# First layer's modulation in two steps of eight blocks per group, with own buffers for each half, and partial sums turned by transposes

## The chip, the cores and the metric

The kernel runs on one core of a Trainium2 chip. The metric is the device time of one execution in microseconds; the figure given is the median of three runs. A core has TensorE (matrix products), VectorE and ScalarE (elementwise work), GpSimd, and SyncE, which here only issues DMAs. The engines run their own instruction queues in order and wait for one another by semaphores.

## The reference

Two layers of a diffusion backbone work on 256 latent and 256 context tokens of width 2048. Each layer modulates its input by the conditioning vectors, multiplies it by one combined projection, runs a spatial gating path and an attention path, and ends with an output projection and a gated residual. What the change touches is the modulation of layer 0: shift and scale of 2048 features each, for two conditioning vectors, and the projection that consumes them.

```python
def rms_norm(x, w):
    xf = x.astype(jnp.float32)
    y = xf * lax.rsqrt(jnp.mean(xf * xf, axis=-1, keepdims=True) + EPS)
    return (y * w.astype(jnp.float32)).astype(x.dtype)

def modulation(cond, w_mod, b_mod):
    m = jax.nn.silu(cond) @ w_mod + b_mod
    m = m.reshape(-1, 1, 3 * D_MODEL)
    return jnp.split(m, 3, axis=-1)
...
        shift, scale, gate = modulation(c, w_mod[layer], b_mod[layer])
        shift_c, scale_c, gate_c = modulation(c_ctx, w_mod[layer], b_mod[layer])
        h = rms_norm(x, norm_w[layer]) * (1.0 + scale) + shift
        hc = rms_norm(xc, norm_w[layer]) * (1.0 + scale_c) + shift_c
...
        proj = h @ w_in[layer]
        u, v_sgu, za, q, k, v, zb = jnp.split(proj, SPLIT_POINTS, axis=-1)
```

## The kernel before

Every large product runs as three passes over exact splits of both operands (`three`: hi*hi, lo*hi, hi*lo). The order of work on TensorE, SyncE, VectorE and ScalarE is the program's own order.

Layer 0 begins with the key, value and query columns of the projection, 1536 of them, and takes the 2048 contraction rows in nine groups of 128-row blocks: `GROUPS` is (0,), (1,), (2, 3), (4, 5), up to (14, 15). For each group the kernel must first have the shift and scale of its features (a `ModItems` object), then the modulated rows (`rows_h`), and then it multiplies them by the group's three pieces of weights. `run_groups` goes through the groups. Each pass but the first has twelve calls of `group_unit`, u = 0 to 11: for each of three column pieces `ci` and four token tiles `tt`, six products of 512 columns (three where the group has one block) into one of four accumulators of the pool `accp`. VectorE then adds the accumulator to the result in SBUF. `first_group` does the same for group 0 while the context tokens still arrive.

Between the units of group gi the kernel prepares group gi + 1:

- `mod_step` at u = 0, 2, 4 and 6 (`WAVE[0]`): four contraction blocks of the modulation product. Each block's weights are the moving operand, 512 columns (256 for a group of one block), and the two conditioning vectors, padded to 32 columns, are the stationary one. The four blocks of a step write four strips of 32 partitions of one PSUM bank, so four partial sums stand there in the end. After the last step ScalarE copies them to `part`.
- `finish` at u = 8 (`WAVE[1]`): TensorE multiplies 128-column pieces of `part` with the constant `sel`, which adds the four strips and turns features onto the partitions; `mod_ab` makes the factors A and B.
- `rows_h` at u = 10 and 11: the modulated rows of the latent and the context tokens.
- `load_w` at u = 2, 4 and 7 (`LOADS`) issues the three weight pieces of group gi + 1, 512 KB each; `split_w` at u = 2, 3 and 8 (`SPLITS`) makes hi by a cast on ScalarE and, a tick later, lo by a subtraction on VectorE. The split at u = 2 is that of the third piece of group gi, the other two belong to group gi + 1.

SyncE issues all these loads. The modulation weights, 4 MB for a group of two blocks, come in pieces of 512 KB into the six rotating buffers `raw`, which `load_w` uses for its third piece too; `mod_load` keeps at most `MOD_AHEAD` of them counted ahead, and one step (`MOD_BIG`) has a buffer of its own. Of the loads that stand before `load_w(gi + 1, 0)` in a pass, those issued at u = 0 and u = 2 are modulation pieces for the steps that follow. The pool tag `pt`, two buffers of 1 MB, is first used by attention, after the last group.

Of the kernel before, what the change touches and what calls it, by code (L numbers as in the profile page):

```python
# [49 lines left out]
FIRST = ((0, 1), 0, (3, 4, 6), 5, (9, 11), (7, 11))  # L50
LOADS = (2, 4, 7)
SPLITS = (2, 3, 8)
WAVE = ((0, 2, 4, 6), 8, 10)
AHEAD = {'raww': 3, 'rawm': 3}
MOD_AHEAD = 3
MOD_BIG = (8,)
# [7 lines left out]
def mixer_kernel(ctx: ExitStack, tc: tile.TileContext, a, out):  # L64
    """Tokens are ordered latent (tiles 0, 1), context (tiles 2, 3).

    Every large product runs as three float32r passes over exact splits of both
    operands: v = hi + lo with hi = float32r(v), and a*b = hi*hi + hi*lo + lo*hi.
    """
# [56 lines left out]
    sel = const([P, 2], "sel")  # L126
    G.dma_start(out=sel, in_=a["sel"])
# [9 lines left out]
    # the conditioning vectors behind their SiLU, in rows: (quarter, stream, element)  # L137
# [23 lines left out]
    def consts_task(l, L):  # L161
        """What the mixer needs beside the modulation: norm weights, and those of queries and keys with the rotation."""
        vn = const([P, 8], "vn")
        nc.sync.dma_start(out=vn, in_=a["vnt"][l])
        L["vn"] = vn
        cs = t2([P, 2, 2, HD], "cs")
        nc.sync.dma_start(out=cs, in_=a["cossin"])
        ws = []
        for key, wname in (("k", "k_norm_w"), ("q", "q_norm_w")):
            w = const([P, HD], "w" + key)  # L170
            load_bc(w, a[wname][l])
            ws.append(w)
        yield 8
        V.tensor_scalar(out=ws[1], in0=ws[1], scalar1=HD ** -0.5, scalar2=None, op0=ALU.mult)
        for key, w in zip("kq", ws):
            C = const([P, NLAT, HD], "C" + key)
            Sn = const([P, NLAT, HD], "S" + key)
            wb = view(w, "p (o d) -> p o d", o=1).broadcast_to([P, NLAT, HD])
            V.tensor_tensor(out=C, in0=cs[:, 0], in1=wb, op=ALU.mult)
            ws4 = view(w, "p (x h d) -> p x h d", x=2, h=2)  # L180
            for h in range(2):
                for n in range(NLAT):
                    V.tensor_tensor(
                        out=view(Sn[:, n], "p (x h d) -> p x h d", x=2, h=2)[:, :, h],
                        in0=view(cs[:, 1, n], "p (x h d) -> p x h d", x=2, h=2)[:, :, h],
                        in1=ws4[:, :, 1 - h], op=ALU.mult)
                yield 1
            L["w" + key], L["C" + key], L["S" + key] = w, C, Sn

# [7 lines left out]
    def split_piece(rs, at_once, mem=None):  # L197
        """float32r parts of two contraction blocks; the second part follows a tick later unless at once."""
# [13 lines left out]
    class ModItems:  # L212
        """Shift and scale of n blocks of features from block kt0, for both streams, on the tensor engine: four
        steps over the contraction, then a finish."""

        def __init__(self, L, kt0, n):
            self.L, self.kt0, self.n, self.wd, self.raw = L, kt0, n, 2 * n * P, {}

        def load(self, g, mem=None):
            kt0, n, wd = self.kt0, self.n, self.wd  # L220
            per = 1024 // wd
            self.raw[g] = []
            for k in range(4 * g, 4 * g + 4, per):
                r = view(mem() if mem else raw2(None), "p a (b n) -> p (a b) n", n=wd)
                o = 2 * P * D * kt0 + k * P * wd
                nc.sync.dma_start(out=r, in_=view(a["w_mod0"][o:o + per * P * wd], "(k p n) -> p k n", p=P, n=wd))
                self.raw[g] += [r[:, j, :] for j in range(per)]

        def compute(self, g):
            wd = self.wd  # L230
            if g == 0:
                self.ps = misc("mod")
            for j in range(4):
                T.matmul(self.ps[32 * j:32 * j + 32, :wd], sc[:, 4 * g + j, :], self.raw[g][j],  # L234
                         start=(g == 0), stop=(g == 3))
            if g == 3:
                self.part = t2([P, 512], "part")[:, :wd]
                (S.copy if PART_ACT else V.tensor_copy)(self.part, self.ps[:, :wd])

        def finish(self):  # L240
            n = self.n
            p2 = view(misc("ab")[:, 0:8], "p (j c) -> p j c", c=2)
            for j in range(2 * n):
                T.matmul(p2[:, j, :], self.part[:, j * P:(j + 1) * P], sel, start=True, stop=True)
            mod_ab(self.L, p2[:, :n], p2[:, n:2 * n], self.kt0, n)
# [10 lines left out]
    def mod_task(row0, ng, ns, pace, finish):  # L256
        """ng groups of 256 columns of the modulation product on the vector engine, columns on the partitions.
        finish gets the sums [P, 2 * ng, ns] of the first ns streams."""
# [42 lines left out]
    def mod_rest():  # L301
        """The gates of the first layer, then the second layer's modulation."""
# [5 lines left out]
    # A task is a generator; it yields how many units of the main stream pass before it goes on.  # L308
# [5 lines left out]
    def later(k, f):  # L314
        """Emit f's instructions k + 1 ticks from now."""
# [27 lines left out]
    class Job:  # L343
        """512 output columns: units of main-stream work for each piece of two contraction blocks."""
# [38 lines left out]
    class Stream:  # L383
        """The pieces of a list of jobs in order, loaded and split ahead of their use."""
# [50 lines left out]
    def head_norm(q, n, kind):  # L435
        """q [P, n, 128] in place: divide by the root mean square of each head."""
# [41 lines left out]
    def attention_task(L, kv, qa, units, done):  # L478
        """kv [P, 4, 512]: k heads in columns 0..255, v heads in 256..511. qa[hf] [P, nt, 4, 128]: queries in,
        transposed attention output in the same place."""  # L480
# [152 lines left out]
    def gate_evac(func, buf, ntok, mix=None):  # L633
        """buf [P, nt, 4, 128] *= func(product), block fb of 128 features; split if that was the last factor."""
# [13 lines left out]
    def to_mix(buf, mix, fb):  # L648
        """Split block fb of a finished [P, nt, 4, 128] buffer into float32r parts [P, 4, tokens]."""
# [6 lines left out]
    def sgu_v(L, buf, hf, nt):  # L656
        """buf [P, nt, 4, 128] gets the position-mixed value path, transposed."""
# [57 lines left out]
    def modulate(L, kt, stream, xs, rb, hi, lo):  # L715
        """hi + lo = xs * rb * A + B for one block of 128 features; returns what makes lo."""
# [7 lines left out]
    # column starts of the combined projection  # L724
    U0, VS0, ZA0, Q0, KV0, ZB0 = 0, 1024, 2048, 3072, 4096, 4608

    # ================= layer 0 =================
    L0 = layer_consts(0)
    mods = [ModItems(L0, g[0], len(g)) for g in GROUPS]
    mseq = [(m, g) for m in mods for g in range(4)]  # L730
    mpos = [0, 0]

    def mod_load():
        """Loads modulation weights ahead, into at most MOD_AHEAD buffers."""
        while mpos[0] < len(mseq):
            m, g = mseq[mpos[0]]
            own = mpos[0] in MOD_BIG
            if not own and mpos[1] + m.n > MOD_AHEAD:
                return
            if own:  # L740
                t_ = big([P, 4, NTOK], s="mod")
                m.load(g, iter((t_[:, :2], t_[:, 2:])).__next__)
            else:
                m.load(g)
                mpos[1] += m.n
            mpos[0] += 1

    def mod_step(m, g):
        m.compute(g)
        if m is not mods[0] and mseq.index((m, g)) not in MOD_BIG:  # L750
            mpos[1] -= m.n
        mod_load()
# [4 lines left out]
    def stats(s, g):  # L757
        """Mean squares of a stream's tokens; the tensor engine adds up over the features on the partitions."""
# [20 lines left out]
    for g in range(4):  # L779
        if g % 2 == 0:  # L780
            first = big([P, 4, NTOK], s="mod")
        mods[0].load(g, lambda: first[:, 2 * (g % 2):2 * (g % 2) + 2, :])
    mpos[0] = 4
# [26 lines left out]
    def rows_h(gi):  # L810
        """Space for the modulated rows of a group, and the steps that make them."""
# [17 lines left out]
    mod_load()  # L829
    mod_step(mods[0], 0)  # L830
    mod_step(mods[0], 1)
    dg0 = stats_rows(0)
    mod_step(mods[0], 2)
    mod_step(mods[0], 3)
# [10 lines left out]
    def first_group():  # L845
        """The latent tokens' products run while the other stream arrives."""
        for u, (ci, tt) in enumerate([(ci, 2 * s + t) for s in range(2) for ci in range(3) for t in range(2)]):
# [4 lines left out]
            if u in FIRST[2]:  # L852
                mod_step(mods[1], FIRST[2].index(u))
            if u == FIRST[3]:
                dg1 = stats_rows(1)
            if u == 6:
                mod_step(mods[1], 3)
# [28 lines left out]
    def run_groups():  # L886
        first_group()
        for gi in range(1, len(GROUPS)):
            nxt = mods[gi + 1] if gi + 1 < len(GROUPS) else None
            make = []  # L890
            for u in range(3 * NT):
                if nxt and u in WAVE[0]:
                    mod_step(nxt, WAVE[0].index(u))
# [67 lines left out]
    # the residual stream is read again for the output projection  # L961
# [42 lines left out]
    # layer 1 jobs  # L1004
# [78 lines left out]
    # last columns of layer 0: the latent tokens end first, so that their next layer can begin  # L1083
# [18 lines left out]
    def next_task(s):  # L1102
        """The next layer's input of one stream, from the new residual stream."""
# [63 lines left out]
    # ================= layer 1 =================  # L1167
# [6 lines left out]
def _layout(inputs):  # L1174
# [22 lines left out]
    # constants of the shapes alone  # L1197
# [33 lines left out]
```

## Time and profile before

| | |
|---|---|
| median of three runs | 1196.34 us (1195.98 to 1197.25) |
| span of the profiled execution, first to last instruction | 1194.6 us |
| TensorE (PE) busy | 1169.5 us, 98% |
| VectorE (DVE) busy | 908.9 us, 76% |
| ScalarE (ACT) busy | 521.5 us, 44% |
| moved by DMA | 247.52 MB, 207 GB/s in the mean |

The profile is of one execution, and its time is the span and what lies before and after it; no clock of that execution but the span is given, and the median of the runs is 1.74 us above it. PE, PEld, DVE, ACT and POOL are the engines' names in the rows (PEld is TensorE's loading of the stationary operand), SPq is SyncE's queue. Matrix products are pipelined: a record of 0.39 us is followed by the next one's start after 0.23 us, so starts are to be compared, not ends. A fp32 product that isn't split leaves two records. A row of windows gives the stretch and its length, then the busy time (and the count of instructions) of PE, PEld, DVE, ACT and POOL, the granted clock of TensorE (1.00 is 2.4 GHz), the busy share of the DMA engines and their GB/s.

### The profile page before, as it was taken

Reading aid. Unit: us, or ns where it says so; the run is one execution under the profiler, and the core shown is the slowest. Engines: PE = TensorE matmul, PEld = TensorE weight load, DVE = VectorE, ACT = ScalarE, POOL = GpSimd, SP = SyncE. Lnnn points to the kernel's source line nnn. Section 1 sums busy time; section 2 is a strip of 40 time slices with the busy share of each in tenths; the row PEclk is TensorE's granted clock in tenths of the full one; section 3 lists DMA queues with packets and bytes.
Section 4 is the critical chain, followed back from the end, with each engine's and each line's share of the span. In section 5 each row is a group of like instructions: output and inputs, shape, how many; then the busy total and the mean of one; then the engine's idle time right before and its main releaser. Section 6 shows DMA issues by size and latency. Waiting matters only on the chain.

```text
span 1194.6 us, 18034 instructions
## 1 busy us (share of the span) xinstructions
PE 1169.5 (98%) x6656; PEld 991.5 (83%) x6656; DVE 908.9 (76%) x1930; ACT 521.5 (44%) x992; POOL 47.0 (4%) x48
## 2 busy tenths in 40 slices
PE   4999999999999999999999999999999999999998
PEld 2566667888888888888888888987888989999998
DVE  5767769878887777989988998778558687767544
ACT  4422225565555432242332232146366777645332
POOL 1000001011000000010100000000011000000000
PEclk9999999999999999999999999999999999999999
DMA  9986772446354657677786666646456666677752
GB/s 334 345 291 246 264 290 99 145 130 191 117 159 141 178 179 224 192 232 219 253 299 215 215 203 195 229 118 220 139 161 200 216 195 220 207 258 252 236 190 89
DMA packets 132184, 247.52 MB, mean 207 GB/s; under 512 B 8912, under 2 KB 19696, under 8 KB 132096
## 3 DMA queue, kind: packets, MB, share of 16 engines
q1 hardware_dynamic: 130880, 242.08, 62.3%
q0 software_dynamic: 1216, 4.29, 1.0%
q8 instruction: 52, 0.85, 0.3%
q14 instruction: 36, 0.29, 0.1%
HBM read 244.23 MB, written 2.11 MB: 206 GB/s over the span
## 4 chain that ended last, share of the span: by engine, by line
PE 89%; DVE 4%; ACT 3%; issue 1%; SPq 1%; POOL 1%; DMA 1%; POOLq 0%; ACTq 0%; DVEq 0%
PE acc L339 27%; PE acc L341 26%; PE acc L340 26%; PE mod L234 2%; PE tp L544 1%; DVE lo L205 1%; PE sg L686 1%; PE s L341 1%; ACT hi L202 1%; PE o L340 1%; PE o L341 1%; PE o L339 1%; POOL rs L429 1%; PE s L340 1%; PE s L339 1%
## 5 line engine op out<-in xcount | busy, mean ns | idle before, releaser
L202 ACT CAST hi<-raw 128x1024 fp32r<-128x1024 f32 (+1 forms) x242 | 250.7, 1036 | 395.6 <-PE acc L340 283.2
L205 DVE TENSOR_TENSOR lo<-raw,hi 128x1024 fp32r<-128x1024 f32 (+1 forms) x242 | 292.2, 1208 | 126.8 <-ACT hi L202 126.5
L284 DVE SCALAR_TENSOR_TENSOR junk<-raw,scb 128x512 f32<-128x512 f32 x448 | 308.1, 688 | 14.5 <-DMA raw<-in_w_modt 5.5
L339 PE MATMUL acc<-hh,hi 128*128 128x512 f32 x384 | 152.6, 397 | 0.0
L341 PE MATMUL acc<-hh,lo 128*128 128x512 f32 x384 | 149.8, 390 | 0.0
L340 PE MATMUL acc<-hl,hi 128*128 128x512 f32 x384 | 149.8, 390 | 0.0
L339 PE MATMUL acc<-hi,hh 128*128 128x512 f32 x320 | 131.0, 409 | 3.1 <-ACT hh L720 3.1
L341 PE MATMUL acc<-hi,hl 128*128 128x512 f32 x320 | 125.6, 393 | 0.0
L340 PE MATMUL acc<-lo,hh 128*128 128x512 f32 x320 | 125.3, 392 | 0.0
L339 PE MATMUL acc<-h,hi 128*128 128x256 f32 x384 | 110.3, 287 | 1.0 <-ACT s L660 1.0
L341 PE MATMUL acc<-h,lo 128*128 128x256 f32 x384 | 108.6, 283 | 0.0
L340 PE MATMUL acc<-h,hi 128*128 128x256 f32 x384 | 108.5, 283 | 0.0
L339 PE MATMUL acc<-mh,hi 128*128 128x512 f32 (+1 forms) x304 | 106.5, 350 | 0.0
L341 PE MATMUL acc<-mh,lo 128*128 128x512 f32 (+1 forms) x304 | 106.4, 350 | 0.0
L340 PE MATMUL acc<-ml,hi 128*128 128x512 f32 (+1 forms) x304 | 106.4, 350 | 0.0
L339 PEld LDWEIGHTS acc<-hi,hh 128*128 128x128 f32 x320 | 60.5, 189 | 38.8 <-issue 14.7
L341 PEld LDWEIGHTS acc<-hh,lo 128*128 128x128 f32 x384 | 72.1, 188 | 15.4
L340 PEld LDWEIGHTS acc<-hl,hi 128*128 128x128 f32 x384 | 72.3, 188 | 13.5
L339 PEld LDWEIGHTS acc<-hh,hi 128*128 128x128 f32 x384 | 72.2, 188 | 13.5
L429 POOL TENSOR_TENSOR rs<-rs,nhalf 128x4 f32<-128x4 f32 (+1 forms) x36 | 40.9, 1137 | 892.7 <-DVE rs L428 892.7
L340 PE MATMUL acc<-lo,h 128*128 128x512 f32 x192 | 75.3, 392 | 0.7 <-DVE lo L205 0.3
L339 PE MATMUL acc<-hi,h 128*128 128x512 f32 x192 | 75.7, 394 | 0.0
(163 smaller groups left out, 2166.6 us busy)
## 6 DMA issues: line engine op xcount, KB each, us to landing
raw<-in_w_in SPq DMA_DIRECT2D x173, 512.0 KB, 4.4
raw<-in_w_modt SPq DMA_DIRECT2D x128, 512.0 KB, 4.7
raw<-in_w_out SPq DMA_DIRECT2D x64, 512.0 KB, 5.0
raw<-in_w_mod SPq DMA_DIRECT2D x58, 512.0 KB, 6.2
scb<-crow SPq DMA_DIRECT2D x12, 512.0 KB, 6.0
xT<-in_xT SPq DMA_DIRECT2D x8, 512.0 KB, 7.8
x<-in_xT POOLq DMA_DIRECT2D x4, 1024.0 KB, 11.0
mod<-in_w_mod SPq DMA_DIRECT2D x6, 512.0 KB, 7.7
```

Of the source, the lines that this page charges most:

```text
L202: S.copy(hi, rs)
L205: V.tensor_tensor(out=lo, in0=rs, in1=hi.bitcast(F32), op=ALU.subtract)
L234: T.matmul(self.ps[32 * j:32 * j + 32, :wd], sc[:, 4 * g + j, :], self.raw[g][j], start=(g == 0), stop=(g == 3))
L284: V.scalar_tensor_tensor(out=junk, in0=rs[i][:, b_, :], scalar=1.0, in1=scbs[q][:, s_, :], op0=ALU.mult, op1=ALU.mult, accum_out=part[:, 2 ...
L339: T.matmul(ps, lhi, rhi, start=first, stop=False)
L340: T.matmul(ps, lhi, rlo, start=False, stop=False)
L341: T.matmul(ps, llo, rhi, start=False, stop=last)
L429: G.tensor_tensor(out=r, in0=r, in1=nhalf[:, :n], op=ALU.pow)
L544: T.transpose(out=tp[:, c * P:(c + 1) * P], in_=p_[:, c * P:(c + 1) * P], identity=ident)
L686: T.matmul(ps[:, tt * P:(tt + 1) * P], buf[:, tt, g, :], ws[:, g, :], start=True, stop=True)
```

## The change

The modulation of each group now runs in two steps of eight contraction blocks, at u = 2 and u = 6. Blocks k and k + 4 write the same strip, so there are still four partial sums. Each half has its own buffers: the first half of a group's weights lies in the two `pt` buffers (two DMAs of 1 MB), the second in four `raw` buffers (four DMAs of 512 KB). For group 1, with one block, it is one DMA of 1 MB into a buffer of `u8` and two of 512 KB. `mod_step(i, h)` computes half h of group i and then loads half h of group i + 1 into the buffers that it has just read. `finish` turns `part` by transposes, 128 columns each, and VectorE adds the four strips by one reduce out of PSUM. The constant `sel` and its DMA go. `LOADS` and `SPLITS` stay as they are. Comments and docstrings that the diff removes are left out here.

```diff
-FIRST = ((0, 1), 0, (3, 4, 6), 5, (9, 11), (7, 11))
+FIRST = ((0, 1), 0, 4, 5, (9, 11), (7, 11))
 LOADS = (2, 4, 7)
 SPLITS = (2, 3, 8)
-WAVE = ((0, 2, 4, 6), 8, 10)
+WAVE = ((2, 6), 8, 10)
-MOD_AHEAD = 3
-MOD_BIG = (8,)
...
-    sel = const([P, 2], "sel")
-    G.dma_start(out=sel, in_=a["sel"])
...
+        def load(self, mem):
+            wd, k = self.wd, len(self.raw)
+            per = mem.shape[1] // wd
+            r = view(mem, "p (k n) -> p k n", n=wd)
+            o = 2 * P * D * self.kt0 + k * P * wd
+            nc.sync.dma_start(out=r, in_=view(a["w_mod0"][o:o + per * P * wd], "(k p n) -> p k n", p=P, n=wd))
+            self.raw += [r[:, j, :] for j in range(per)]
+
+        def compute(self, ks):
             wd = self.wd
-            if g == 0:
+            if ks[0] == 0:
                 self.ps = misc("mod")
-            for j in range(4):
-                T.matmul(self.ps[32 * j:32 * j + 32, :wd], sc[:, 4 * g + j, :], self.raw[g][j],
-                         start=(g == 0), stop=(g == 3))
-            if g == 3:
+            for k in ks:
+                j = 32 * (k % 4)
+                T.matmul(self.ps[j:j + 32, :wd], sc[:, k, :], self.raw[k], start=k < 4, stop=k >= KT - 4)
+            if ks[-1] == KT - 1:
                 self.part = t2([P, 512], "part")[:, :wd]
                 (S.copy if PART_ACT else V.tensor_copy)(self.part, self.ps[:, :wd])
 
         def finish(self):
             n = self.n
-            p2 = view(misc("ab")[:, 0:8], "p (j c) -> p j c", c=2)
+            pt = misc("ab")[:, :self.wd]
             for j in range(2 * n):
-                T.matmul(p2[:, j, :], self.part[:, j * P:(j + 1) * P], sel, start=True, stop=True)
-            mod_ab(self.L, p2[:, :n], p2[:, n:2 * n], self.kt0, n)
+                T.transpose(out=pt[:, j * P:(j + 1) * P], in_=self.part[:, j * P:(j + 1) * P], identity=ident)
+            ab = small([P, 4, 2], "ab")[:, :2 * n]
+            V.tensor_reduce(out=ab, in_=view(pt, "p (j a b) -> p j b a", a=4, b=32)[:, :, 0:2, :], axis=AX.X, op=ALU.add)
+            mod_ab(self.L, ab[:, :n], ab[:, n:2 * n], self.kt0, n)
...
-    def mod_step(m, g):
-        m.compute(g)
-        if m is not mods[0] and mseq.index((m, g)) not in MOD_BIG:
-            mpos[1] -= m.n
-        mod_load()
+    def mod_load(i, h):
+        m = mods[i]
+        for _ in range(1 if h == 0 and m.n == 1 else 2 * m.n if h else 2):
+            if h:
+                mem = view(raw2(None), "p a b -> p (a b)")
+            else:
+                mem = view((big if i == 1 else ptile)([P, 4, 512], F32, s="mod"), "p a b -> p (a b)")
+            m.load(mem)
+
+    def mod_step(i, h, ahead=1):
+        mods[i].compute(range(8 * h, 8 * h + 8))
+        if i + ahead < len(mods):
+            mod_load(i + ahead, h)
...
-    mod_load()
-    mod_step(mods[0], 0)
-    mod_step(mods[0], 1)
+    mod_load(1, 0)
+    mod_load(1, 1)
+    mods[0].compute(range(8))
     dg0 = stats_rows(0)
-    mod_step(mods[0], 2)
-    mod_step(mods[0], 3)
+    mods[0].compute(range(8, KT))
...
-            if u in FIRST[2]:
-                mod_step(mods[1], FIRST[2].index(u))
+            if u == FIRST[2]:
+                mod_load(2, 0)
+                mods[1].compute(range(8))
...
             if u == 6:
-                mod_step(mods[1], 3)
+                mod_step(1, 1)
...
                 if nxt and u in WAVE[0]:
-                    mod_step(nxt, WAVE[0].index(u))
+                    mod_step(gi + 1, WAVE[0].index(u))
```

## Rows read from the trace of the kernel before

**Rows 1.** The page, busy time of the engines, share of the span, instructions.

```profile
PE 1169.5 (98%) x6656; PEld 991.5 (83%) x6656; DVE 908.9 (76%) x1930; ACT 521.5 (44%) x992; POOL 47.0 (4%) x48
```

**Rows 2.** Windows, the pass over group 4.

```profile
96.54:118.72 22.18, 22.18 (x113) 14.72 (x113) 15.01 (x27) 5.44 (x8) 0.00 (x0) 1.00 0.79 273
```

**Rows 3.** Timeline of TensorE, group 4, u = 2: start, length, engine, line, operation.

```profile
100.17 0.39 PE L341 MATMUL acc<-hi,hl 128*128 128x512 f32 x1
100.49 1.07 PE L234 MATMUL mod<-raw,scb 128*32 128x512 f32 x8
101.48 0.50 PE L339 MATMUL acc<-hi,hh 128*128 128x512 f32 x1
101.82 0.39 PE L340 MATMUL acc<-lo,hh 128*128 128x512 f32 x1
102.05 0.39 PE L341 MATMUL acc<-hi,hl 128*128 128x512 f32 x1
```

**Rows 4.** Timeline of TensorE, first group: one step of four blocks, then two together.

```profile
27.02 0.64 PE L234 MATMUL mod<-raw,scb 128*32 128x256 f32 x8
27.59 0.50 PE L339 MATMUL acc<-hi,hh 128*128 128x512 f32 x1
...
30.50 1.07 PE L234 MATMUL mod<-raw,scb 128*32 128x256 f32 x16
31.50 0.71 PE L704 MATMUL rsb<-dg,ones 128*128 128x128 f32 x4
```

**Rows 5.** Timeline of TensorE, group 4, u = 8: the finish.

```profile
112.01 0.39 PE L341 MATMUL acc<-hi,hl 128*128 128x512 f32 x1
112.24 0.95 PE L244 MATMUL ab<-sel,part 128*128 128x2 f32 x8
113.05 0.49 PE L339 MATMUL acc<-hi,hh 128*128 128x512 f32 x1
```

**Rows 6.** Timeline of TensorE, attention: four transposes between products.

```profile
224.23 0.40 PE L341 MATMUL acc<-hi,hl 128*128 128x512 f32 x1
224.46 0.60 PE L544 MATMUL tp<-ident,p 128*128 128x128 f32 x4
224.82 0.48 PE L339 MATMUL acc<-hi,hh 128*128 128x512 f32 x1
```

**Rows 7.** Timeline of VectorE, group 4, from u = 3 on.

```profile
105.66 1.22 DVE L205 TENSOR_TENSOR lo<-raw,hi 128x1024 fp32r<-128x1024 f32 x1 [1.79 <-ACT hi L202]
106.81 0.68 DVE L884 TENSOR_TENSOR kv<-acc,kv 128x512 f32<-128x512 f32 x1
...
113.22 0.16 DVE L252 TENSOR_TENSOR modB<-ab,bm 128x4 f32<-128x4 f32 x1
```

**Rows 8.** Timeline of ScalarE, group 4: modulated rows, cast of the split at u = 3.

```profile
97.50 0.91 ACT L720 ACTIVATE hh<-hm,modB 128x256 fp32r<-128x256 f32 x2 [1.55 <-DVE hm L719]
...
104.58 1.04 ACT L202 CAST hi<-raw 128x1024 fp32r<-128x1024 f32 x1 [5.23 <-PE acc L341]
```

**Rows 9.** Timeline of SyncE's queue, group 4: two issues, modulation and weights.

```profile
97.63 0.37 SPq L226 DMA_DIRECT2D raw<-in_w_mod  x1
98.05 0.46 SPq L803 DMA_DIRECT2D raw<-in_w_in  x1
```

**Rows 10.** Issue to landing by source line: issues at 97.63, 98.05 and 75.86.

```profile
DMA to landing us min/median/max: 3.7/3.7/3.7
...
DMA to landing us min/median/max: 4.5/4.5/4.5
...
DMA to landing us min/median/max: 5.9/5.9/5.9
```

**Rows 11.** Timeline of TensorE: an early product, and products after a long wait.

```profile
23.24 0.63 PE L339 MATMUL acc<-hi,hh 128*128 128x512 f32 x1
...
208.69 0.41 PE L520 MATMUL qt<-ident,qa 128*128 128x128 f32 x2 [1.77 <-DVE rs L428]
...
209.17 0.39 PE L340 MATMUL acc<-lo,hh 128*128 128x512 f32 x1
```

More of the change, by code (lines that the diff above doesn't have):

```diff
@@ L216, in __init__ @@
         def __init__(self, L, kt0, n):
[L217 to L229, printed above, removed]
+            self.L, self.kt0, self.n, self.wd, self.raw = L, kt0, n, 2 * n * P, []
+        def load(self, mem):
[6 more added lines that the diff above has]
+        def compute(self, ks):
             wd = self.wd
-            if g == 0:
+            if ks[0] == 0:
                 self.ps = misc("mod")
-            for j in range(4):
-                T.matmul(self.ps[32 * j:32 * j + 32, :wd], sc[:, 4 * g + j, :], self.raw[g][j],
-                         start=(g == 0), stop=(g == 3))
-            if g == 3:
+            for k in ks:
+                j = 32 * (k % 4)
+                T.matmul(self.ps[j:j + 32, :wd], sc[:, k, :], self.raw[k], start=k < 4, stop=k >= KT - 4)
+            if ks[-1] == KT - 1:
                 self.part = t2([P, 512], "part")[:, :wd]
@@ L729, in mixer_kernel @@
     mods = [ModItems(L0, g[0], len(g)) for g in GROUPS]
[L730 to L742, printed above, removed]
-            else:
-                m.load(g)
-                mpos[1] += m.n
-            mpos[0] += 1
-    def mod_step(m, g):
-        m.compute(g)
-        if m is not mods[0] and mseq.index((m, g)) not in MOD_BIG:
-            mpos[1] -= m.n
-        mod_load()
+    def mod_load(i, h):
[3 more added lines that the diff above has]
+                mem = view(raw2(None), "p a b -> p (a b)")
+            else:
+                mem = view((big if i == 1 else ptile)([P, 4, 512], F32, s="mod"), "p a b -> p (a b)")
[4 more added lines that the diff above has]
+            mod_load(i + ahead, h)
     sq, sums0 = [], small([P, 512], "sums", bufs=1)
@@ L781, in mixer_kernel @@
             first = big([P, 4, NTOK], s="mod")
-        mods[0].load(g, lambda: first[:, 2 * (g % 2):2 * (g % 2) + 2, :])
-    mpos[0] = 4
+        mods[0].load(view(first[:, 2 * (g % 2):2 * (g % 2) + 2, :], "p a b -> p (a b)"))
     for g in range(4):
```

## The prediction

> **What bounds the kernel now.** I read the page first, then the windows by stage, then the timeline of TensorE through one wave, and last the queues that feed it. TensorE works for 98% of the span [rows 1], so a change counts only where it shortens or holds up TensorE. Call one pass of `run_groups` over a group a wave, its twelve `group_unit` calls units 0 to 11, and `load_w(gi + 1, 0)` W0. In the window of wave 4 TensorE is busy for the whole stretch, 22.18 of 22.18 us [rows 2]; waves 2, 3 and 5 to 7 have the same length within 0.1 us, and wave 1, with half the products, is as dense. So no load, split or sum holds it up there: each microsecond taken from TensorE in a wave is a gain, each new wait a loss. Before wave 1, at the start of the kernel, it does wait for others.
>
> **What TensorE gains.** A step of four blocks for two feature blocks: the last product before it starts at 100.17, the first after it at 101.48 and the second at 101.82, where two more products at their pitch of 0.23 would have ended the same distance at 100.63 [rows 3]. It costs 1.19 us, of which 0.09 is waited before it (0.32 instead of 0.23) and 0.11 after it (0.34 instead of 0.23). What lies inside shows in the first group, with half the columns: four blocks take 0.57 us to the next product, eight in a row 1.00 [rows 4]. Four more cost 0.43 there, and a step of their own would have cost 0.57 + 0.32 + 0.34 - 0.46 = 0.77. Merging two steps therefore saves 0.34. With 512 columns four more blocks cost twice 0.43, so a step of eight costs 1.19 + 0.86 = 2.05 us (and 0.99 + 0.86 = 1.86 from its start to the next product). A wave merges twice: 0.68.
>
> The finish now takes 1.04 us from the last product to the next [rows 5]; four transposes of the same size take 0.59 where attention does them [rows 6]. That saves 0.45. The new reduce on VectorE (32 numbers a partition) is bounded by the sum over 4 elements, 0.16, and by the one over 512, 0.68 [rows 7]; I take 0.2, as it is nearest to the small one. It lies behind transposes that end at unit 8, and the factors are wanted at unit 10, two units of 1.38 us later, so it costs nothing; without that cover it would cost its 0.2. Waves 1 to 7 each have a modulation group: 7 x (0.68 + 0.45) = 7.9 us gained. The steps and finishes of the first two groups lie in the start, where TensorE then waits for row statistics anyway: I count them as nothing (at most 0.34 + 2 x 0.23). The lost DMA of `sel` is off the path.
>
> **What the new order of loads costs.** SyncE issues in program order and stops at a buffer that isn't free. Before, W0 went out at 98.05, behind one modulation load of 97.63, while TensorE was still in unit 0 [rows 9]; TensorE's step at unit 2 came at 100.49. After the change, `mod_step` at unit 2 runs its eight blocks and then reloads the two `pt` tiles that those blocks have just read: two transfers of 1 MB, and W0 stands behind them in the same queue. The first `pt` tile is free when four blocks have ended, 1.07 us after the start A of the step [rows 3]. A load on an idle queue landed after 3.7 us, W0 issued 0.42 later after 4.5 [rows 9, 10]: 1.3 us per 512 KB behind 2.4 us of latency. So W0 (512 KB behind 2 MB) lands at A + 1.07 + 2.4 + 5 x 1.28 = A + 9.9; before, it landed 98.05 + 4.5 - 100.49, at A + 2.1.
>
> Who waits for it: the cast of `split_w(gi + 1, 0)` on ScalarE, emitted at unit 3. Before, it began at 104.58, when unit 3 had ended and its buffer came free [rows 8]. Behind it on VectorE stands `lo` (105.66), and behind `lo` the sum of unit 3 (106.81, 0.68 long) [rows 7]: 2.9 us from cast to the end of that sum. There are four accumulators, so unit 7 can't begin before unit 3's is added up. After the change that is A + 9.9 + 0.1 + 2.9 = A + 12.9. TensorE alone would come to unit 7 at A + 1.86 (step) + 1.48 + 3 x 1.38 + 0.09 + 1.86 (the step at unit 6) + 1.48 = A + 10.9. TensorE stands for 2.0 us in each wave that loads a following modulation group: waves 2 to 6 make 10.0. Wave 7 has nothing more to load, and W0 goes out early there.
>
> The Trainium skill, "DMA: Bandwidth & Descriptors", Specifications, puts the limit of the memory at about 358 GB/s for a core. By that figure 512 KB would take 1.46 us, W0 would land 0.9 later, and six waits would cost 5.4 more; the trace's 1.3 us is about 400 GB/s and the measurement decides.
>
> Wave 1 has units of three products (0.69), so TensorE is at unit 7 sooner: A + 1.86 + 0.80 + 3 x 0.69 + 0.09 + 1.86 + 0.80 = A + 7.5. It stands for 5.4. Then VectorE is late with the next group's rows. From A + 12.9 it has four sums (0.6 each, as a successor starts some 0.07 before the end: `lo` of 1.22 is followed after 1.15), the reduce and the factors (0.6), another `lo` (1.15), two more sums (1.2), and a product; with the activation behind it that is another 1.0, since two such activations take 0.91 [rows 7, 8]: A + 19.3 for the first `hh`. TensorE would come to wave 2 at A + 12.9 + 5 x 0.69 + 0.36 (finish) + 0.11 = A + 16.8. That is 2.4 more; bounds nothing and 3. Wave 1 loses 7.8.
>
> W0 took 5.9 us to land in wave 3, and as long in wave 2, where it took 4.5 in wave 4 [rows 10]; two in seven were late. Before, nothing waited for that. Now such 1.3 us falls on TensorE: none of six to all of six is 0 to 7.8; two in seven of six make 2.2. I take 1.5, between that and nothing.
>
> Sum: -7.9 + 10.0 + 7.8 + 1.5 = +11.4 us. The profiled span of 1194.6 becomes 1206.0; the median of the runs, 1196.34, is 1.7 above that span, and becomes 1207.7. I say 1207.5.
>
> **The rivals.** *The late load is hidden.* If W0 lands by A + 7.9, unit 7 finds its accumulator, only the gain is left, and the time is 1196.3 - 7.9 = 1188.5. For it speaks that the waves have no wait now and that the DMA engines are busy for only 0.79 of wave 4 [rows 2]; against it, the issue at A + 1.07 and the latency leave 4.4 us for 2.5 MB that take 6.4 at the rows' pace. A scheduler that issues W0 first, or a queue that serves it at once, would also do it. Chance 0.10.
>
> *The waits are half of that.* If the chain from issue to sum is 1 us shorter, the waits are 4.4 in wave 1 and 1.0 in five others, and without late landings the loss nearly equals the gain: 9.4 - 7.9 = +1.5, 1197.8, or 1200.2 with wave 1's second wait. Chance 0.08.
>
> *The waits grow, or TensorE slows after them.* Late landings in all six waves make 1207.7 - 1.5 + 7.8 = 1214. And the first products of the kernel took 0.63 us where later ones take 0.39 [rows 11]: TensorE began at 1.2 GHz, by that duration, for some seven products, which costs 7 x 0.24 = 1.7; in wave 4 the granted clock reads 1.00, 2.4 GHz [rows 2]. If each wait threw it back there, six waits cost 10 us, 1217.7; in wave 1 alone, 1209.4. The nearest row speaks against the short waits: after 1.77 us of standing at 208.69 the next products took 0.39 as before [rows 11]; for the 5.4 us of wave 1 there is no row. The Trainium skill, "TensorE: Matmul & The Clock Gate", "Why this matters for your kernels", says that an idle gap between bursts of matmuls sends the clock from 2.4 back to 1.2 GHz if it is long enough; the 1.77 us row shows no such fall, and no run here shows it for a longer one. Chance 0.16.
>
> **How the numbers follow.** The forecast has 0.66. A run of this kernel can tell about 0.2%, 2.4 us, from no change. Faster is the first rival, 0.10. Of the second rival 0.05 lies within 2.4 us of 1196.3, the rest above: same 0.05, slower 0.66 + 0.16 + 0.03 = 0.85. The low end of the range takes the waits at 1.5 us in five waves, 5.0 in wave 1 and nothing else: -7.9 + 7.5 + 5.0 = +4.6, 1201. The high end takes late landings in all waves and the slow products in wave 1: 11.4 - 1.5 + 7.8 + 1.7 = +19.4, cut to 1215, since both at full size are unlikely together. Below lie the first rival and most of the second.
>
> **What would show it.** In the windows of waves 1 to 6 TensorE must no longer be busy throughout: one wait per wave, before the first product of unit 7, released by VectorE's sum, some 2 us long (5 in wave 1), and a cast on ScalarE that waits for the DMA of `in_w_in`. The waves should last 23.1 us where they last 22.2, the last of them 21.0. Each step must show as sixteen records with about 1.86 us to the next product, each finish as four. If the waves last 21.0 with no wait, the late load was hidden and I am wrong on the sign; if the wait comes before the finish or before a step instead, the mechanism is another.

## The result and the profile after

The changed kernel takes 1223.82 us (median; 1221.28 to 1228.08) where the kernel before takes 1196.74 in the same comparison: ratio 1.0226 [1.0212, 1.0241]. The forecast was 1207.5 in a range of 1201 to 1215. The sign was right, the size far too small.

The profiled execution has a span of 1226.3 us. The page's first two parts and its chain, against [rows 1]: TensorE's busy time has hardly grown, and its clock has an 8 in two of the first slices, where the page before has a 9 in all.

```profile
PE 1174.3 (96%) x6624; PEld 997.9 (81%) x6624; DVE 909.0 (74%) x1939; ACT 521.4 (43%) x992; POOL 46.9 (4%) x47
...
PEclk9899989999999999999999999999999999999999
...
PE 82%; DMA 6%; DVE 5%; ACT 4%; SPq 2%; issue 1%; POOL 1%; ACTq 0%; POOLq 0%; DVEq 0%
```

The waits of TensorE from wave 1 to the end of the waves (engine, what waited, what released it: total us, times, longest):

```profile
PE acc L337 <- DVE kv L874: 23.8, 7, 7.2
...
PE acc L337 <- ACT hh L718: 1.0, 1, 1.0
```

L874 is VectorE's sum of a unit. The waits before unit 7 are 7.2 us in wave 1 and 2.9, 3.6, 4.1, 2.8 and 2.7 in waves 2 to 6; wave 7 has none; the seventh of the row, 0.5 us, stands before unit 6 of wave 1, and the one for `hh` at the start of wave 2. TensorE's timeline in wave 2, from the step at unit 2 to the wait (start, duration, in brackets the idle time before and its releaser), answers to [rows 3]:

```profile
65.32 1.92 PE L230 MATMUL mod<-mod,scb 128*32 128x512 f32 x16
67.17 0.50 PE L337 MATMUL acc<-hi,hh 128*128 128x512 f32 x1
...
72.88 1.92 PE L230 MATMUL mod<-raw,scb 128*32 128x512 f32 x16
...
76.02 0.39 PE L339 MATMUL acc<-hi,hl 128*128 128x512 f32 x1
79.34 0.79 PE L337 MATMUL acc<-hi,hh 128*128 128x512 f32 x1 [2.94 <-DVE kv L874]
79.93 0.63 PE L338 MATMUL acc<-lo,hh 128*128 128x512 f32 x1
80.36 0.63 PE L339 MATMUL acc<-hi,hl 128*128 128x512 f32 x1
```

Unit 6 ends with the product of 76.02, and unit 7 starts at 79.34. The chain behind it stands in the timelines of SyncE's queue, ScalarE and VectorE, and in the landing times of the three issues of 66.44, 67.30 and 67.72:

```profile
66.44 1.23 SPq L221 DMA_DIRECT2D mod<-in_w_mod  x2
67.72 1.09 SPq L793 DMA_DIRECT2D raw<-in_w_in  x2
...
76.38 1.04 ACT L198 CAST hi<-raw 128x1024 fp32r<-128x1024 f32 x1 [10.32 <-DMA raw<-in_w_in]
...
77.46 1.23 DVE L201 TENSOR_TENSOR lo<-raw,hi 128x1024 fp32r<-128x1024 f32 x1 [7.88 <-ACT hi L198]
78.60 0.68 DVE L874 TENSOR_TENSOR kv<-acc,kv 128x512 f32<-128x512 f32 x1
```

```profile
DMA to landing us min/median/max: 5.5/5.5/5.5
DMA to landing us min/median/max: 7.6/7.6/7.6
DMA to landing us min/median/max: 8.6/8.6/8.6
```

The two 1 MB transfers land at 71.9 and 74.9, W0 behind them at 76.3; the cast follows at 76.38, `lo` at 77.46, the sum of unit 3 ends at 79.28, and unit 7 begins. This is the forecast's chain, about 1 us later than it said. The second thing to see is the duration behind the wait: 0.63 and a pitch of 0.43 us instead of 0.39 and 0.23. The windows of the stretch before and behind the wait, of waves 2, 3 and 5, and of the low clock in wave 1 (columns as in [rows 2]; the seventh figure is the granted clock):

```profile
75.00:79.30 4.30, 1.40 (x6) 0.78 (x5) 1.84 (x3) 1.53 (x2) 0.00 (x0) 1.00 1.05 392
79.34:82.72 3.38, 3.38 (x10) 2.69 (x11) 2.15 (x4) 0.37 (x1) 0.00 (x0) 0.50 1.05 387
82.74:91.10 8.36, 8.36 (x39) 6.67 (x37) 7.55 (x18) 3.32 (x6) 0.00 (x0) 1.00 0.08 30
65.32:91.10 25.78, 22.85 (x110) 15.69 (x109) 15.56 (x29) 5.98 (x9) 0.00 (x0) 0.93 0.62 224
91.10:117.64 26.54, 22.92 (x110) 15.72 (x109) 15.00 (x28) 5.34 (x9) 0.00 (x0) 0.94 0.62 218
144.60:171.55 26.95, 24.19 (x109) 16.69 (x109) 16.38 (x39) 5.01 (x9) 0.00 (x0) 0.87 0.60 215
...
52.05:58.88 6.83, 3.09 (x9) 2.57 (x10) 4.74 (x10) 2.58 (x3) 0.00 (x0) 0.50 0.97 359
```

Behind each of the six waits of this execution (in waves 1, 5 and 6 already within it) the clock reads 0.50, which is 1.2 GHz, for 3.41 or 6.83 us: 27.3 us in all, of which TensorE stands for 4.7, most of it in wave 1. Working 22.6 us at half clock loses half of that, 11.3. The waves last 25 to 27 us where the forecast had 23.1.

### The profile page after: what moved, and what is told of

Read it like the earlier page. It is cut to its first block, busy times and chain, and to the rows that moved or that the text cites. A ratio compares the mean times of both kernels' runs of the same rounds, so it can differ in the third digit from the quotient of the medians.

```text
span 1226.3 us, 17941 instructions
## 1 busy us (share of the span) xinstructions
PE 1174.3 (96%) x6624; PEld 997.9 (81%) x6624; DVE 909.0 (74%) x1939; ACT 521.4 (43%) x992; POOL 46.9 (4%) x47
## 4 chain that ended last, share of the span: by engine, by line
PE 82%; DMA 6%; DVE 5%; ACT 4%; SPq 2%; issue 1%; POOL 1%; ACTq 0%; POOLq 0%; DVEq 0%
PE acc L337 25%; PE acc L339 24%; PE acc L338 24%; DMA raw<-in_w_in 5%; DVE lo L201 2%; PE mod L230 1%; ACT hi L198 1%; PE tp L542 1%; PE sg L684 1%; DMA mod<-in_w_mod 1%; PE s L339 1%; PE o L338 1%; POOL rs L427 1%; PE o L339 1%; PE o L337 1%
## 5 line engine op out<-in xcount | busy, mean ns | idle before, releaser
L201 DVE TENSOR_TENSOR lo<-raw,hi 128x1024 fp32r<-128x1024 f32 (+1 forms) x242 | 292.4, 1208 | 169.6 <-ACT hi L198 169.3
L337 PE MATMUL acc<-hi,hh 128*128 128x512 f32 x320 | 134.2, 419 | 28.3 <-DVE kv L874 23.8
L338 PE MATMUL acc<-lo,hh 128*128 128x512 f32 x320 | 129.2, 404 | 0.0
L339 PE MATMUL acc<-hi,hl 128*128 128x512 f32 x320 | 129.0, 403 | 0.0
L337 PEld LDWEIGHTS acc<-hi,hh 128*128 128x128 f32 x320 | 62.6, 196 | 56.1 <-DVE kv L874 27.3
```

Of the source, the lines that this page charges most:

```text
L201: V.tensor_tensor(out=lo, in0=rs, in1=hi.bitcast(F32), op=ALU.subtract)
L337: T.matmul(ps, lhi, rhi, start=first, stop=False)
L338: T.matmul(ps, lhi, rlo, start=False, stop=False)
L339: T.matmul(ps, llo, rhi, start=False, stop=last)
```

## The experiments

The theory after the result: W0 stands in SyncE's queue behind 2 MB, its cast and `lo` hold up the sum of unit 3 on VectorE, TensorE waits for that before unit 7, and then works at half clock for a while. Rivals: the transposes and the reduce cost the time; the loads have become slower; the clock falls for another reason than the waits. Each comparison is with the kernel before on the same chip.

**The changed kernel again** (`after_again`), without an edit.

> The changed kernel once more, as the yardstick of the three kernels run beside it on the same chip. Late load of W0 with falls of the granted clock (theory): about 1222 us, in the passes over groups 1 to 6 one wait before unit 7 of 2.9 to 4.2 us (7 in the first) and a stretch at 0.5 after each. Rival, that the profiled execution had only a slow memory: landings of 512 KB return to 1.27 to 1.30 us apart, the waits shrink to 2.0 us and the time to about 1208.

1222.92 us, ratio 1.0221 [1.0199, 1.0242]. The waits repeat (6.5, 2.7, 2.9, 3.9, 2.9 and 2.85 us), but in the profiled execution the clock fell only after those of wave 1, 4 and 6, for 13.7 us in all, and its span is 7.7 us shorter than the one shown above. That fits the changed kernel's own spread of 7 us: how often the clock falls differs from execution to execution (the mean granted clock of the eight executions is 0.987 to 0.994).

**W0 ahead of the reloads** (`w0_early`): the one load is issued a unit earlier, the rest of the change stays.

```diff
-LOADS = (2, 4, 7)
+LOADS = (1, 4, 7)
```

> One number: the first weight piece of the next group is issued at unit 1, ahead of the reload of the two 1 MB buffers. Theory (the 2 MB in front of it make it late, all loss hangs on that): the waits of groups 2 to 6 go, group 1 keeps about 2 us because its loads are still queued from the start, the granted clock stays at 1.00; 1196.7 - 7.9 + 2 + 1 = about 1192 us. Rival (the larger transfers or the shared buffers slow all loads, or the reduce and transposes are to blame): the waits stay, above 1208 us.

1198.76 us, 1.0016 [1.0007, 1.0026]: 24 of the 26 us are gone, though the 1192 expected was not reached. Waits of TensorE from wave 1 on, then the windows of waves 1 and 3:

```profile
PE acc L337 <- ACT hh L718: 4.1, 1, 4.1
...
PE acc L337 <- DVE kv L874: 1.3, 1, 1.3
```

```profile
39.35:61.80 22.45, 17.00 (x79) 10.42 (x78) 15.19 (x30) 6.14 (x10) 0.00 (x0) 0.85 0.89 328
82.80:103.86 21.06, 21.06 (x110) 14.59 (x109) 14.90 (x28) 5.46 (x9) 0.00 (x0) 1.00 0.78 275
```

Waves 2 to 6 have no wait and last 21.0 us (one 21.5), 1.1 less than before [rows 2]. What is left is in wave 1: 22.45 us where its work takes 14.2. There the second piece now stands behind the 2 MB, and the rows of group 2 come late. So the place of one issue in the queue explains nearly all of the loss.

**The splits later** (`split_late`): W0 lands late, but no sum stands behind it until unit 6.

```diff
-SPLITS = (2, 3, 8)
+SPLITS = (2, 6, 8)
```

> One number: the loads stay as in the changed kernel, W0 still lands some 11 us after the step at unit 2, but its cast and subtraction stand at unit 6 instead of unit 3. Theory (what hurts is not the late load but that ScalarE and VectorE stand behind it in their queues and hold an accumulator): no wait in groups 2 to 6, about 5 us left in group 1 with a fall of the clock; 1196.7 - 7.9 + 5 + 2 + 1 = about 1197 us. Rival (TensorE lacks data): about 1222 us as before.

1204.05 us, 1.0058 [1.0041, 1.0075]. Waits from wave 1 on:

```profile
PE acc L337 <- DVE qa L874: 4.1, 1, 4.1
PE acc L337 <- ACT hh L718: 3.9, 4, 1.5
```

The loads are as in the changed kernel, yet no wait stands before unit 7: it is not the load but the work queued behind it that held TensorE. The expectation missed by 7 us. In wave 1 the same chain, emitted three units later, held up a later sum for 4.1 us; in four waves the next group's rows (`hh`), which VectorE makes behind the split, came late by up to 1.5 us, 3.9 in all; and the clock read 0.50 for 10.2 us, from within the first wait on. One wait was spread over other places.

**The wait filled with products** (`fill_wait`): nothing that the output uses changes; before unit 7 TensorE does products that nobody reads.

```diff
+                if u == 7 and gi <= len(GROUPS) - 3:
+                    fill = misc("fill")
+                    for _ in range(28 if gi == 1 else 12):
+                        T.matmul(fill, H[GROUPS[gi][0]][0][:, 0:P], wpcs[gi, 1][0][:, 0, :], start=True, stop=True)
                 group_unit(gi, *divmod(u, NT))
```

> The changed kernel with products that nothing reads, 12 of 512 columns (28 in group 1) before unit 7 of groups 1 to 6, where TensorE would only stand. Theory (of the loss some 12 us are the half rate after each wait): the granted clock stays at 1.00, the waits end no later, and the time falls by 10 to 12 us below the changed kernel on the same chip, to about 1211. Rival (the half rate costs little, because VectorE is the bound there anyway): no gain, or a loss of up to 3 us for the added products.

1216.27 us, 1.0162 [1.0147, 1.0178]. Mean granted clock, the products that fill the wait of wave 2, the first behind them, and the wave's window:

```profile
core 0: 1214.8 us, clock 1.000
```

```profile
75.14 2.91 PE L904 MATMUL fill<-hi,hh 128*128 128x512 f32 x12
78.05 0.50 PE L337 MATMUL acc<-hi,hh 128*128 128x512 f32 x1
78.39 0.39 PE L338 MATMUL acc<-lo,hh 128*128 128x512 f32 x1
```

```profile
64.22:88.26 24.04, 24.04 (x121) 16.75 (x120) 15.37 (x29) 5.95 (x9) 0.00 (x0) 1.00 0.66 241
```

The chain to unit 7 is as late as before, but TensorE does not stand, and the clock does not fall: more work, 6.65 us less time than in the unedited kernel of the same comparison (some 3 us either way, by the two intervals; 10 to 12 was expected). The mean granted clock of its four executions is 0.999 or 1.000. So standing is what lowers the clock, and 6.65 us is about what that costs in a typical execution, where the first profile makes it 11.3; it is a net figure, as `fill_wait` waits 2.1 us for `hh` at the start of wave 2 where `after_again` waits 0.3.

**The kernel before once more** (`before_look`), and **the new finish alone** (`finish_only`): the kernel before with the transposes and the reduce in place of `sel`, and its old steps and loads.

```diff
-    sel = const([P, 2], "sel")
-    G.dma_start(out=sel, in_=a["sel"])
...
             for j in range(2 * n):
-                T.matmul(p2[:, j, :], self.part[:, j * P:(j + 1) * P], sel, start=True, stop=True)
+                T.transpose(out=pt[:, j * P:(j + 1) * P], in_=self.part[:, j * P:(j + 1) * P], identity=ident)
```

> The kernel before, profiled again beside the others. In the profiles of the changed kernel 512 KB land 1.355 us apart, already in loads that the change leaves alone, and 1.27 to 1.30 in the first profile of before. If that pace belongs to the chip or the execution, this run too shows about 1.355, and still no wait of TensorE in groups 1 to 7 (span 1194 to 1196). If the change causes it, this run shows 1.27 to 1.30.

> The kernel before with one part of the change alone: transposes and the reduce on VectorE in place of the products with sel. Theory (0.45 us less on TensorE for each of seven groups, the reduce hidden): 0.26% faster, 3.1 us, and no new wait. Rival (the reduce lengthens the way to the factors and the rows come late, as they do in the changed kernel before some groups): no gain, or up to 1.5 us slower.

The kernel before ran in 1196.67 us, with dense waves. The finish alone: 1196.04, 0.9992 [0.9983, 1.0001]. It costs nothing, so that rival falls; but it gave less than expected. Its waves are shorter as expected; its start is 0.8 us later (first product of the second half of the first group at 34.59 instead of 33.78), as in the changed kernel, and its 512 KB loads land 1.35 us apart instead of 1.28. The experiments with the pad, below, ask why.

**All weight loads first** (`w_first`, and with it the later split, `w_first_split_late`): the changed kernel with its three weight pieces issued ahead of the modulation reloads.

```diff
-LOADS = (2, 4, 7)
+LOADS = (0, 1, 2)
...
             for u in range(3 * NT):
+                if u in LOADS:
+                    load_w(gi + 1, LOADS.index(u))
                 if nxt and u in WAVE[0]:
                     mod_step(gi + 1, WAVE[0].index(u))
...
-                if u in LOADS:
-                    load_w(gi + 1, LOADS.index(u))
```

> The changed kernel with all three weight pieces of the next group issued at units 0, 1 and 2, each ahead of the reloads of modulation buffers. Theory (the loss left in w0_early is group 1 alone, where the second piece stands behind 2 MB while the queue is still full from the start): about 2 us of wait left before unit 7 of group 1, no fall of the clock, 1196.8 - 7.9 + 2 + 1 = about 1192 us. Rival (the early load of a whole group of modulation weights costs its 4 MB at the start in any order): the loss of group 1 moves to the step at unit 2 of group 2, and the time stays at about 1198.

> As w_first, and the cast of the first piece at unit 6 instead of 3. Theory: the wait of group 1 goes too, TensorE is dense from group 1 on, about 1190 us, 0.6% faster than before. Rival: as for w_first, about 1198.

`w_first`: 1194.99 us, 0.9983 [0.9974, 0.9991]; `w_first_split_late`: 1195.61, 0.9990 [0.9981, 0.9999]. No wait before unit 7 is left worth naming; the later split buys nothing: 2.8 us of waiting for `hh` at the start of wave 2 against 2.1 without it. Both lie above what was expected, again with the loads 1.35 us apart.

**Thirty-two bytes** (`after_pad`, `before_shift`, `finish_pad`, `w_first_pad`). The constant `sel`, [128, 2], takes 32 bytes of each partition. Without it the large buffers that come behind it in SBUF start 32 bytes past a multiple of 64 bytes instead of at one (by the program's own allocation; a trace shows no addresses). The edit puts an unused constant of the same size there: into three kernels without `sel`, which restores the old places, and into the kernel before, which shifts them.

```diff
+    V.memset(const([P, 2], "pad"), 0.0)
     ones = const([P, P], "ones")
```

> The changed kernel with an unused constant of two elements a partition where sel stood. It takes 32 bytes a partition, so all large buffers lie again at multiples of 64 bytes, as in the kernel before; without it they lie 32 bytes off. Theory (the offset slows every load): 512 KB land 1.27 to 1.30 us apart as before, the start ends at 33.8 again, the waits before unit 7 shrink to 2.0 to 2.5 us (5.4 in group 1), the granted clock falls less often; about 1208 to 1212. Rival (the chip or the changed loads are slow, not the addresses): 1.355 us and 1222 as before.

> The kernel before with the same unused constant added, which moves its large buffers 32 bytes off the multiples of 64. Theory: 512 KB land 1.345 to 1.355 us apart, the loads of the start 1.5 instead of 1.35, the start ends about 0.9 us later, and the time grows by 1 to 2 us. Rival: no change, 1.28 and 1196.8.

> The transposes and the reduce alone, with the large buffers at multiples of 64 bytes. Theory (in finish_only the gain of 3.2 us on TensorE was eaten by the slower loads of the start): 1197.1 - 3.2 = about 1193.9 us, 0.27% faster. Rival (the reduce delays the rows): 1196 as in finish_only.

> All weight pieces ahead of the reloads, and the large buffers at multiples of 64 bytes. Theory: the start is 1 to 2 us shorter than in w_first and the wait at the step of group 2 smaller, about 1191 to 1192 us, faster than before by 0.4 to 0.5%. Rival: 1195 as in w_first.

One window at the start, 12.6 to 21.7 us, when the loads run without a break, in the kernel before (`before_look`), the kernel before shifted, the changed kernel and the changed kernel with the pad (the last figure is GB/s):

```profile
12.60:21.70 9.10, 6.54 (x44) 3.27 (x44) 5.16 (x15) 2.18 (x5) 0.93 (x2) 1.00 1.08 389
```

```profile
12.60:21.70 9.10, 6.99 (x44) 3.54 (x44) 4.61 (x14) 1.78 (x4) 1.07 (x2) 1.00 1.09 355
```

```profile
12.60:21.70 9.10, 6.78 (x42) 3.02 (x42) 4.68 (x15) 1.78 (x4) 0.79 (x2) 1.00 1.09 355
```

```profile
12.60:21.70 9.10, 6.65 (x43) 3.25 (x38) 4.84 (x15) 3.03 (x6) 0.71 (x1) 1.00 1.08 389
```

The pace follows the place of the buffers: 389 GB/s in the old place, 355 shifted, whichever kernel it is. In time, each against the kernel before on its own chip: `before_shift` 1197.96, 1.0009 [1.0000, 1.0018], 1.0 us more; `finish_pad` 1194.21, 0.9979 [0.9970, 0.9988], 1.7 us better than `finish_only`; `w_first_pad` 1192.3, 0.9962 [0.9949, 0.9976], 2.5 us better than `w_first`. But `after_pad` takes 1223.57, 1.0220 [1.0206, 1.0234], as long as without the pad, where 1208 to 1212 was expected. Its start is faster: the second half of the first group begins at 32.95 instead of 34.63, of which 0.8 lie before TensorE's first product (11.96 instead of 12.77) and 0.9 behind it. Its waits are as long as in `after_again`:

```profile
PE acc L338 <- DVE kv L875: 21.6, 6, 6.2
```

So the slower loads don't make the waits of the changed kernel, and that rival falls for the waves; with the pad, too, W0 lands at A + 10.6 to A + 11.8 (A is the start of the step at unit 2, as in the prediction).

**The 1 MB transfers cut in two** (`after_pad_512`): `after_pad`, with the `pt` buffers loaded by four DMAs of 512 KB.

```diff
+    V.memset(const([P, 2], "pad"), 0.0)
...
-            m.load(mem)
+            if h or i == 1:
+                m.load(mem)
+            else:
+                m.load(mem[:, :1024])
+                m.load(mem[:, 1024:])
```

> As after_pad, with the two pt buffers loaded in four transfers of 512 KB instead of two of 1 MB; order and gates are the same. Theory (the prediction's sum is right once the pieces are those of its rows): W0 lands at A + 9.9 instead of A + 10.8, the waits before unit 7 are 1.9 to 2.2 us, and if TensorE's clock then stays at 1.00 after most of them, the time is about 1208 to 1211. Rival (the first megabyte of a burst is slow whatever its pieces): W0 at A + 10.8, waits of 2.6 to 3.8 us, about 1222. If the waits are 2 us and the clock falls all the same: about 1217.

1219.91 us, 1.0180 [1.0164, 1.0196]. The 1208 to 1211 of its theory was missed. W0 lands at A + 10.0 to A + 10.5 in four waves and 1.3 later in waves 3 and 4; the waits are 5.8, 2.2, 3.5, 3.7, 2.4 and 2.0 us. Against `after_pad`, cutting the transfers brings the landing in those four waves 0.25 to 0.6 us nearer to the forecast's A + 9.9. The windows of waves 2, 3, 5 and 6 of this kernel:

```profile
62.56:87.68 25.12, 22.90 (x109) 15.70 (x108) 15.61 (x29) 5.95 (x9) 0.00 (x0) 0.93 0.60 230
87.68:114.94 27.26, 23.72 (x110) 16.36 (x109) 14.99 (x28) 5.34 (x9) 0.00 (x0) 0.87 0.59 212
142.34:166.50 24.16, 21.61 (x110) 14.37 (x109) 15.74 (x38) 4.72 (x9) 0.00 (x0) 1.00 0.66 240
166.50:189.79 23.29, 21.30 (x110) 14.50 (x109) 15.39 (x29) 5.98 (x9) 0.00 (x0) 1.00 0.88 312
```

After 2.2 and 3.5 us of standing the clock fell, after 2.4 and 2.0 it didn't. Waves 5 and 6, at full clock, last 24.16 and 23.29 us; the second is nearly the wave of 23.1 us that the forecast described.

**The best version** (`best`): `w_first_pad` with the last split of a pass moved from unit 8 to unit 11, behind the next group's rows.

```diff
-SPLITS = (2, 3, 8)
+SPLITS = (2, 3, 11)
```

> w_first_pad with the second piece's cast and subtraction at unit 11 instead of 8, behind the next group's rows. Theory (the 2.2 us that are left before group 2 are VectorE's queue, in which a subtraction of 1.2 us stands ahead of the rows): that wait falls by about 1.1 us and the clock no longer falls behind it, 1190 to 1191 us. Rival (the wait comes from the sums in that queue): 1192 as in w_first_pad.

1191.1 us, 0.9949 [0.9937, 0.9962], faster than both kernels. The wait for `hh` before wave 2 is 0.9 us instead of 2.1. Its waits from wave 1 on, and the windows of waves 1, 2 and 5:

```profile
PE acc L338 <- ACT hh L719: 0.9, 1, 0.9
PE acc L338 <- DVE qa L875: 0.6, 1, 0.6
```

```profile
39.38:54.97 15.59, 14.65 (x80) 8.72 (x79) 12.45 (x27) 4.45 (x9) 0.00 (x0) 1.00 1.05 407
54.97:76.02 21.05, 21.05 (x109) 14.59 (x108) 15.29 (x28) 5.98 (x9) 0.00 (x0) 1.00 0.92 334
118.10:139.13 21.03, 21.03 (x110) 14.59 (x109) 16.59 (x38) 5.01 (x9) 0.00 (x0) 1.00 0.83 295
```

The gain of the merged steps and the short finish is all there: 21.04 us a wave against 22.18 [rows 2].

## Why the prediction was right in sign and wrong in size

**The gain was right.** 0.68 + 0.45 = 1.13 us a wave was forecast; the dense waves of `w0_early` and `best` are 1.12 to 1.15 shorter. Seven make the forecast's 7.9; `best` gets 6.1 of it, and 1.5 goes in its two waits. A step of eight takes 1.85 us to the next product (1.86 forecast), a finish 0.58 (0.59).

**The mechanism was right.** W0 behind the two reloads, the cast, `lo`, the sum of unit 3 and unit 7 came in that order, 3.0 us from landing to unit 7 (3.0 forecast). `w0_early` takes the first link away and the loss with it, `split_late` the link between `lo` and the sum.

**The step that failed is the price of a wait.** The forecast took a wait to cost its own length, because after the 1.77 us wait of [rows 11] the next products took 0.39 us, and gave 0.16 to the rival in which the waits grow or TensorE slows down after them; both happened. That row was one wait; the new ones are 2.7 us and longer. The rival had 1.7 us for each fall, and a stretch of 3.41 us at half clock costs 1.7, in part by luck: 7 x 0.24 was worked out from durations, and by starts (0.43 instead of 0.23) the seven products cost 1.4. Its sum of 10 us for six falls became 11.3 in the profiled execution, as two of the six stretches are twice as long, and some 6.7 in a typical one, where not every wait brings a fall. The Trainium skill, "TensorE: Matmul & The Clock Gate", "Why this matters for your kernels", says that a long enough gap between bursts of matmuls brings the clock down; the windows at 0.50 after the waits, and `fill_wait` at 1.000, agree with that. How long is long enough no run settles: gaps of 2.0 to 2.9 us stand on both sides. The forecast set the rival aside on the strength of that one row.

**The second term mis-sized is W0's landing.** Forecast A + 9.9, measured A + 10.8 to A + 12.1 in waves 2 to 6. The transfers were priced at 1.28 us per 512 KB, which puts the first megabyte at A + 6.0 and the second 2.56 later; they land at A + 6.4 to A + 6.9 and 2.7 to 3.4 later. In waves 3 and 4 W0 is 0.7 and 1.1 us later than in wave 2, the jitter that the forecast had counted at 1.5 in all. In wave 1 loads of the start are still queued, the first megabyte lands at A + 7.8 and W0 at A + 12.3. From start to start, less the pitch of 0.23, the waits of waves 2 to 6 sum to 16.9 us instead of 10.0, that of wave 1 to 7.35 instead of 5.4, and the one that follows it to 1.1 instead of 2.4: 25.35 instead of 17.8 + 1.5.

**What was not foreseen** is the later start: 0.9 us, by the place of the buffers, which the forecast had at nothing ("the lost DMA of `sel` is off the path" is true, the lost 32 bytes were not looked at). Nor was the short wait before unit 6 of wave 1, 0.6 us in the same count.

The sum for the profiled execution: -7.9 gained, 25.35 + 0.6 waits, 11.3 at half clock, 0.9 at the start, 1.6 after the last finish, together 31.85, where the spans differ by 1226.3 - 1194.6 = 31.7.

**What stays open.** The 1.6 us after the last finish (1016.6 us to the end instead of 1015.0) were not isolated; `finish_only` has 1.5 of them, `w0_early` 0.5. The pad gives the changed kernel its start back and yet not its time; the executions of that kernel differ by up to 7 us with the falls of the clock, which hides 1 to 2 us. Why some bursts land up to 1.3 us later was not settled; a 16 KB transfer of an instruction queue runs in the two late bursts of the first profile and in none of its others, but in `after_again` wave 3 has one too and is not late.

## What to carry to other kernels

When a step is merged, its reload becomes one big burst: ask which small, urgent load stands behind it in the same queue, and issue that one first; here one digit in `LOADS` decided 24 us. Price a new wait on the bounding engine twice, by its length and by what its clock does afterwards, and don't let one shorter wait in the trace stand for longer ones. When a constant goes, look at what moves in SBUF behind it.

## What the runs showed of the hardware

- The destination's place in SBUF sets the pace of the loads: 389 GB/s with the buffers at multiples of 64 bytes, 355 with the same buffers 32 bytes further on, and 512 KB landing 1.28 or 1.35 us apart. It was shown in both directions, on the kernel before and on three kernels without `sel`. It was worth 1.0 to 2.5 us of the time, and nothing that could be told in the changed kernel with its falls of the clock.
- TensorE's granted clock falls to 0.50, 1.2 GHz, after some waits of 2 to 4 us and not after others: it fell after 2.2 us in `after_pad_512` and after 2.1 in `w_first_pad`, and did not after 2.4 and 2.0 in the former, 2.1 in `w_first` and `fill_wait`, and three of 2.7 to 2.9 in `after_again`, while each of 2.7 to 2.9 in the first profile of the changed kernel brought it down. The length of the wait alone doesn't decide it. With unread products in the waits (`fill_wait`) it never fell in the waves.
- Behind the same step, 2 MB in two DMAs of 1 MB had landed at A + 9.2 to A + 10.5 (`after_pad`), in four of 512 KB at A + 8.8 to A + 10.3 (`after_pad_512`), 0.2 to 0.5 us earlier in each wave.
